# Feed-forward mixes queued elsewhere, later sums in the down product, constants and first weights moved: a hybrid decoder block on one core

## The chip, the cores and the metric

The kernel runs on one core of a Trainium2 chip. The metric is the device time of one execution in microseconds; before the change it is 1431.51 us, the median of three runs (1430.36 to 1434.9).

## The reference

One decoder block over T = 1040 positions (16 meta tokens and 1024 tokens), D = 1024, float32. `h` is normalized by `rmsnorm` and multiplied by `w_in`; the product is cut into `u`, `q`, `k`, `v` and two gates. `u` runs through an S5 state-space mixer, `q`, `k`, `v` through differential attention with four heads, both are gated, added and projected by `w_o`. What the change touches most is the feed-forward part:

```python
hn = rmsnorm(h, norm1_g); proj = hn @ w_in
...
h = h + mixed @ w_o
up = rmsnorm(h, norm2_g) @ w_up            # 1024 -> 2 * 2816
a, b = up[..., :D_FF], up[..., D_FF:]
c = a_pad[:, 0:seq] * conv_w[0] + a_pad[:, 1:seq+1] * conv_w[1] + a_pad[:, 2:seq+2] * conv_w[2] + conv_b
h = h + (gelu(c) * b) @ w_down             # 2816 -> 1024
```

## The kernel before

Every product is made of three matmuls per pair of tiles: both operands are split into a high part (fp32r, by ScalarE) and a remainder (by VectorE), and hi·hi, hi·lo and lo·hi are added in PSUM (`mm3_term`, L184, and `mm3`, L132). So each operand costs one ACTIVATE and one VectorE subtraction. `tt` (L94), `ts` (L98, L100), `stt` (L103) and `act` (L106) are helpers; L94 therefore stands for every two-operand VectorE or GpSimd instruction.

**Order.** The framework lays out each engine's instructions ahead of time by a simulated timeline: of the instructions whose inputs its model holds ready, the one written earlier goes first. On the chip each engine then runs its list in that order, and so does each DMA queue; all DMAs of this kernel are issued by SyncE (SP). `keep_in_program_order` puts an instruction behind the one last written for its engine; `issue_after(x)` puts what is written in its block, on the engine of `x`, behind `x`.

**Start** (`start`, L278). Eight row tiles of `hT` (128x1040) are loaded (L301), split with `g1` as scale into `hhi` and `hlo`, and the first two column blocks of `w_in` in pieces (L292). TensorE makes the 16 matmul groups of two u-blocks (six PSUM banks of eight). Then the squares of all eight rows are added into two accumulators `acc`, odd rows on GpSimd and even rows on VectorE; their sum goes through a ones matrix (`rms`, L155) and a chain of ScalarE and VectorE steps to the row `R1`, without which no u-bank can be emptied (`u_evict`). Two more u-blocks follow, then `small_params`, which makes small constants (lambda of the attention, scales) on VectorE, then the S5 constants (`ssm`, beginning with `exp_small` of `ldt`) beside the q, k and v blocks.

**Feed-forward up.** The product `w_up` is made in 2x2 block form with seven products instead of eight (Winograd's form of Strassen). A `Quad` is one set of seven: `part` 0 makes rows of `a` (columns of 258 and 256), `part` 1 rows of `b` (columns of 512). There are 11 quads of each part, in turn; `AHEAD` = 5 quads of part 1 have two of their products made before. `sums` makes four weight sums S1 to S4 on GpSimd from the loaded weights `wraw` (two buffers, L1210). `times` multiplies a result by its gelu row in `c`, on GpSimd; when four such are done, `mix` makes the block sums of the result (four subtractions on GpSimd, each followed by a store to DRAM, L1279 to L1288) for the down product. The rows `c` come from a pool of five.

**Feed-forward down** (`ffn_down`) is again in seven products of 11 steps. Each step loads an activation `act`, splits it (`bop`), splits the weight (`wop`), and makes 12 matmuls of 512 columns (L184). `then(f)` overwrites a block of the weight tile `wd` with a sum that a later product needs; in the first product this is `to_s3`, on VectorE.

Of the kernel before, what the change touches and what calls it, by code (L numbers as in the profile page):

```python
# [8 lines left out]
F32 = mybir.dt.float32  # L9
# [76 lines left out]
class Block:  # L86
# [100 lines left out]
    def build(self):  # L187
        nc, tc, a = self.nc, self.tc, self.a
        if True:
            P = lambda name, bufs=BUFS, **kw: Pool(tc, bufs, name, **kw)  # L190
            cst = self.cst = P("cst")
            self.dr = P("dr", space=bass.MemoryType.DRAM)
            self.wp = P("w")
            self.rowp = P("rows")
            self.tmp = P("tmp")
            self.A = P("A")

            par = cst.tile([128, NPAR], F32, name="par")
            self.par = par
            self.p = {k: par[:, s:e] for k, (s, e) in PAR.items()}  # L200
            self.ident = cst.tile([128, 128], F32, name="ident")
            self.ones = cst.tile([128, 128], F32, name="ones")
            nc.vector.memset(self.ones, 1.0)
            self.blk = cst.tile([128, 128], F32, name="blk")
            nc.vector.memset(self.blk, 0.0)
            nc.vector.memset(self.blk[0:64, 0:64], 1.0)
            nc.vector.memset(self.blk[64:128, 64:128], 1.0)

            d = lambda name, shape: self.dr.tile(shape, F32, name=name)
            self.d_qkv = [d(f"d_qkv{i}", [128, T]) for i in range(12)]  # L210
            self.d_gate = [d(f"d_gate{i}", [128, T2]) for i in range(16)]
            self.d_u = [d(f"d_u{i}", [GB, 16, CH, NJ]) for i in range(4)]
            self.d_y = [d(f"d_y{i}", [CH, 16, GB, NJ]) for i in range(4)]
            self.d_g = [d(f"d_g{i}", [128, T]) for i in range(3)]
            self.d_m1 = [d(f"d_m1{i}", [128, T2]) for i in range(8)]
            self.d_o = [d(f"d_o{i}", [128, T2]) for i in range(H)]
            self.d_h2 = [d(f"d_h2{i}", [128, SEQ]) for i in range(8)]
            self.d_p1, self.d_c11 = ([d(f"d_{n}{i}", [128, HW]) for i in range(AHEAD)] for n in ("p1", "c11"))
            self.d_act = [d(f"d_act{i}", [128, SEQ]) for i in range(NF)]
            self.d_t2, self.d_t3, self.d_t4 = ([d(f"d_t{n}{i}", [128, SEQ // 2]) for i in range(NQ)] for n in (2, 3, 4))  # L220

            x0 = self.x0 = P("X0", {})
            self.pp = P("ps0", {"mm": 8}, space=bass.MemoryType.PSUM)
            self.start()
            for i in (2, 3):
                self.u_block(i)
            self.small_params()
            x0.release()
            self.pp.release()
            self.pp = P("ps1", PBUFS[0], space=bass.MemoryType.PSUM)  # L230
            x = self.x = P("X1")
            ssm = self.ssm()
            step = lambda n: [next(ssm, None) for _ in range(n)]
            step(5)
            for h in range(H):
                for qk in range(2):
                    step(1)
                    self.qk_block(h, qk)
                step(1)
                self.v_block(h)  # L240
            fill = self.fillers()
            tc.keep_in_program_order(nc.scalar.preload_act_table_set(GELU))
            loaded = []
            for n, _ in enumerate(ssm):
                for z in loaded:
                    self.gelu_y(*z)
                loaded = [(i, self.load_branch(i)) for i in ((0, 1), (2,), ())[min(n, 2)]]
                spent = 0.0
                while spent < PRE:
                    spent += next(fill)  # L250
            self.run_later()
            x.release()
            self.pp.release()
            self.pp = P("ps3", PBUFS[1], space=bass.MemoryType.PSUM)
            self.Op = P("O")
            x = self.x = P("X3")
            with tc.manual_schedule(engines={mybir.EngineType.PE}):
                self.attention(fill)
            x.release()
            self.pp.release()  # L260
            self.pp = P("ps4", PBUFS[2], space=bass.MemoryType.PSUM)
            x = self.x = P("X4")
            self.att_out()
            self.w_o()
            x.release()
            self.Op.release()
            self.pp.release()
            self.pp = P("ps5", PBUFS[3], space=bass.MemoryType.PSUM)
            x = self.x = P("X6")
            self.ffn_up()  # L270
            x.release()
            x = self.x = P("X7")
            self.ffn_down()
            for z in (x, self.pp, self.A, self.tmp, self.rowp, self.wp, self.dr, self.cst):
                z.release()


    def start(self):  # L278
# [8 lines left out]
        for _ in range(2):  # L287
            ws.append([self.wp.tile([128, 8, 128], t, tag=n, name="w" + n) for t, n in ((F32, "raw"), (F32R, "hi"), (F32R, "lo"))])

        def weights(i, k0, k1):  # L290
            raw, hi, lo = (z[:, k0:k1] for z in ws[i])
            nc.sync.dma_start(out=raw, in_=a["w_in"][i][:, k0:k1])  # L292
            self.split(raw, hi, lo)

        for k in range(8):
            raw = self.x0.tile([128, T], F32, name=f"hraw{k}")
            hi = self.A.tile([128, T], F32R, tag="A", name="hhi")
            lo = self.A.tile([128, T], F32R, tag="A", name="hlo")
            for n, (c0, cn) in enumerate(C_U if k == 0 else [(0, T)]):
                cs = slice(c0, c0 + cn)  # L300
                nc.sync.dma_start(out=raw[:, cs], in_=a["hT"][k][:, cs])  # L301
                if k == 0 and n == 0:
                    nc.sync.dma_start(out=self.par[:, 0:8], in_=a["par"][:, 0:8])
                    weights(0, 0, 1)
                self.split(raw[:, cs], hi[:, cs], lo[:, cs], self.p["g1"][:, k:k + 1])
            if k == 0:
                weights(1, 0, 1)
                weights(0, 1, 4)
                weights(1, 1, 4)
            if k == 4:  # L310
                nc.sync.dma_start(out=self.par[:, 8:], in_=a["par"][:, 8:])
                nc.sync.dma_start(out=self.ident, in_=a["ident"])
# [14 lines left out]
        for k in range(8):  # L327
            if k < 2:
                self.act(accs[k], raws[k], AF.Square)
            else:  # L330
                self.act(raws[k], raws[k], AF.Square)
                self.tt(accs[k % 2], accs[k % 2], raws[k], ALU.add, eng=nc.gpsimd if k % 2 else None)
        self.E1 = self.rowp.tile([128, T], F32, tag="R", name="E1")
        self.tt(accs[0], accs[0], accs[1], ALU.add)
        self.R1 = self.rms_row(accs[0], T, self.E1)
        self.tap("R1", self.R1)
        for i in range(2):
            self.u_evict(i, ps[i])

# [145 lines left out]
    def small_params(self):  # L485

        p, cst = self.p, self.cst
        lam = p["lam"].rearrange("p (a d) -> p a d", a=4)
        pr = self.x0.tile([128, 2, 64], F32, name="lampr")
        self.tt(pr[:, 0], lam[:, 0], lam[:, 1], ALU.mult)  # L490
        self.tt(pr[:, 1], lam[:, 2], lam[:, 3], ALU.mult)
        s = cst.tile([128, 2], F32, name="lams")
# [17 lines left out]
    def ssm(self):  # L510
# [5 lines left out]
        sgn = q["sgn"]  # L516
        W = 4 * NG
        sm = lambda nm, n: x.tile([128, n], F32, name=nm)
        dt = self.exp_small(q["ldt"], NG, x)
        rr, th = sm("rr", W), sm("th", W)  # L520
        self.tt(rr[:, 0:NG], q["are"], dt, ALU.mult)
        self.tt(th[:, 0:NG], q["aim"], dt, ALU.mult)
# [504 lines left out]

    def ffn_up(self):
        nc = self.nc
        a0 = Quad(self, 0, 0)  # L1030
        bs = [Quad(self, 1, f) for f in range(AHEAD)]
        for q in bs:
# [14 lines left out]
        def whole(q):  # L1047
            q.load(2)
            q.sums()
            q.x12()  # L1050
            q.yz()

# [2 lines left out]
        for f in range(NQ):  # L1055
# [4 lines left out]
            if f < AHEAD:  # L1060
# [3 lines left out]
                    q.fetch()  # L1064
                q.load(2)
                q.sums()
                q.yz(True)
            else:
                q = Quad(self, 1, f)
                q.c = cs[f]  # L1070
                whole(q)

    def arow(self):
        pool, tag = (self.rowp, "R") if self.nar % 3 else (self.x, "ar")
# [20 lines left out]
    def ffn_down(self):  # L1095
# [25 lines left out]
        def to_s4(f):  # L1121
            self.tt(A12(f), A12(f), A21(f), ALU.subtract)

        def product(w, src, then=None):
            tiles = [self.psum("mm", [128, n]) for _ in range(4)]
            for f in range(NQ):
                i = count[0] % 13
# [11 lines left out]
                wh, wl = self.wop(w(f))  # L1139
                for m in range(4):  # L1140
                    self.mm3_term(tiles[m], (wh[:, m], wl[:, m], t[:, 0], t[:, 1]), f == 0, f == NQ - 1)
                if then is not None:
                    then(f)
            return tiles

        def quarter(pool, tag):
# [9 lines left out]
            nc.sync.dma_start(out=self.out[4 * i + m][:, n * half:n * half + n], in_=z)  # L1156

        act = lambda i, half: (lambda f: self.d_act[f + i * NQ][:, n * half:n * half + n])
        tiles = product(A11, act(0, 0), to_s3)
        u, v, w = quarter(self.A, "A"), quarter(self.A, "A"), quarter(x, "w")  # L1160
        for m, ps in enumerate(tiles):
            self.act(u[m], ps, AF.Copy)
# [28 lines left out]
class Quad:  # L1191


    def __init__(self, b, part, f):
        self.b, self.part, self.f, self.nc, self.x = b, part, f, b.nc, b.x
        self.c = None
        self.rows, self.done = [None, None], 0
        if part == 0:
            self.c0, self.n = 0, HW
            self.cuts = (slice(0, HW - 256), slice(HW - 256, HW))  # L1200
# [64 lines left out]
    def times(self, i, half, t):  # L1265
        b = self.b
        o = self.c[i][:, 512 * half:512 * half + 512]
        b.tt(o, o, t, ALU.mult, eng=self.nc.gpsimd)
        self.done += 1
        if self.done == 4:  # L1270
            self.mix()

    def mix(self):

        b, G, f = self.b, self.nc.gpsimd, self.f
        (r0, r1), h0, h1 = self.c, slice(0, 512), slice(512, 1024)
        t3 = self.temp("T")
        b.tt(t3, r1[:, h1], r0[:, h1], ALU.subtract, eng=G)
# [314 lines left out]
```

## Time and profile before

| | |
|---|---|
| median of 3 runs | 1431.51 us (1430.36 to 1434.9) |
| profiled execution | 1431.01 us, span of the trace 1429.2 us |
| busy: TensorE / weight loads / VectorE | 1404.2 (98%) / 1295.4 (91%) / 1029.2 us (72%) |
| busy: ScalarE / GpSimd | 631.9 (44%) / 371.8 us (26%) |
| TensorE clock granted | 0.995 of full, mean |

PE is the matmul engine, DVE is VectorE, ACT ScalarE, POOL GpSimd, SP SyncE; a small q marks an engine's sequencer or queue. Times in a trace count from the start of the span.

### The profile page before, as it was taken

How to read it: one execution, taken by the hardware profiler on the slowest of the kernel's cores; microseconds unless marked ns; L12 is line 12 of the kernel's file. 1: busy time of each engine (PE TensorE's matmuls, PEld its weight loads, DVE VectorE, ACT ScalarE, POOL GpSimd, SP SyncE). 2: the span in 40 equal slices, each digit the busy share in tenths (PEclk: the TensorE clock that was granted, in tenths of full speed). 3: DMA queues.
4: the chain of work that ended last, by engine and by line, in shares of the span. 5: the costliest groups of instructions: out<-in, count | busy, mean ns of one | idle time of the engine just before them, and what ended most of it. 6: DMA issues, size and time to landing. Idle time of an engine off the chain costs nothing.

```text
span 1429.2 us, 22918 instructions
## 1 busy us (share of the span) xinstructions
PE 1404.2 (98%) x8714; PEld 1295.4 (91%) x8714; DVE 1029.2 (72%) x2014; ACT 631.9 (44%) x1177; POOL 371.8 (26%) x242
## 2 busy tenths in 40 slices
PE   8999999999999999999999999999999999999998
PEld 7999999999999999889998999988889997788887
DVE  7998987345646577657366988888666779895574
ACT  6155555444545674433254633333333342444442
POOL 2000000121120111000220166676655557231030
PEclk9999999999999999999999999999999999999999
DMA  5333344471435334656433223333232337944331
GB/s 200 133 78 109 99 131 127 152 199 59 120 100 150 109 106 161 193 182 216 155 130 109 95 80 126 126 126 117 101 107 97 111 112 272 366 134 155 125 119 59
DMA packets 93917, 194.64 MB, mean 136 GB/s; under 512 B 27632, under 2 KB 36976, under 8 KB 93808
## 3 DMA queue, kind: packets, MB, share of 16 engines
q1 hardware_dynamic: 93376, 191.60, 41.5%
q8 instruction: 68, 1.11, 0.3%
q10 hardware_dynamic: 432, 1.60, 0.3%
q14 instruction: 41, 0.34, 0.1%
HBM read 134.88 MB, written 57.10 MB: 134 GB/s over the span
## 4 chain that ended last, share of the span: by engine, by line
PE 88%; DVE 6%; DMA 3%; issue 1%; ACT 1%; POOL 1%; SPq 0%; ACTq 0%; DVEq 0%; POOLq 0%
PE ps_mm L184 40%; PE ps_mm L132 37%; PE po L1463 3%; DVE wop L94 1%; PE s L1427 1%; PE wt L1472 1%; PE s L1428 1%; PE qss L377 1%; DMA wraw<-in_w_up 1%; DMA wd<-in_w_down 1%; PE vps L694 1%; PE yps L736 1%; PE yps L734 0%; PE km L672 0%; DVE crow L103 0%
## 5 line engine op out<-in xcount | busy, mean ns | idle before, releaser
L132 PE MATMUL ps_mm<-B,wop 128*128 128x512 f32 (+2 forms) x2772 | 436.9, 320 | 4.9 <-DVE u L94 3.9
L132 PEld LDWEIGHTS ps_mm<-B,wop 128*128 128x128 f32 x2772 | 395.3, 189 | 46.1 <-ACT wop L106 5.8
L184 PE MATMUL ps_mm<-bop,wop 128*128 128x512 f32 x924 | 216.0, 395 | 2.4 <-DVE bop L94 2.4
L184 PEld LDWEIGHTS ps_mm<-bop,wop 128*128 128x128 f32 x924 | 174.0, 189 | 44.2 <-DVE bop L94 3.3
L184 PE MATMUL ps_mm<-hhi,whi 128*128 128x342 f32 (+2 forms) x432 | 137.5, 329 | 2.5 <-ACT hhi L106 2.4
L184 PE MATMUL ps_mm<-hlo,whi 128*128 128x342 f32 (+2 forms) x432 | 138.8, 322 | 0.0
L184 PE MATMUL ps_mm<-hhi,wlo 128*128 128x342 f32 (+2 forms) x432 | 138.6, 322 | 0.0
L106 ACT ACTIVATE whi<-wraw 128x1024 fp32r<-128x1024 f32 (+3 forms) x62 | 62.1, 1004 | 125.9 <-PE ps_mm L184 46.1
L94 DVE TENSOR_TENSOR wop<-wraw,wop 128x512 fp32r<-128x512 f32 x88 | 97.1, 1108 | 23.5 <-ACT wop L106 23.1
L132 PE MATMUL ps_mm<-hhi,whi 128*128 128x348 f32 (+3 forms) x336 | 112.4, 335 | 0.0
L132 PE MATMUL ps_mm<-hhi,wlo 128*128 128x348 f32 (+3 forms) x336 | 110.0, 327 | 0.0
L132 PE MATMUL ps_mm<-hlo,whi 128*128 128x348 f32 (+3 forms) x336 | 109.2, 325 | 0.0
L94 POOL TENSOR_TENSOR wlo<-wraw,whi 128x1024 fp32r<-128x1024 f32 x18 | 45.2, 2512 | 224.3 <-ACT whi L106 224.3
L1429 DVE CUSTOM_DVE_ANT_0 S<-s,bias 128x348 f32<-128x348 f32 (+9 forms) x120 | 57.9, 484 | 59.6 <-PE s L1428 58.9
L106 ACT ACTIVATE bop<-act 128x512 fp32r<-128x512 f32 x77 | 48.4, 632 | 117.1 <-PE ps_mm L184 117.0
L94 DVE TENSOR_TENSOR wop<-S,wop 128x512 fp32r<-128x512 f32 x66 | 65.3, 990 | 48.1 <-ACT wop L106 48.1
L94 POOL TENSOR_TENSOR crow<-crow,T 128x512 f32<-128x512 f32 x44 | 70.7, 1620 | 97.5 <-DVE T L94 90.8
L106 ACT ACTIVATE wop<-wraw 128x512 fp32r<-128x512 f32 x88 | 54.1, 626 | 91.8 <-DMA wraw<-in_w_up 50.6
L94 DVE TENSOR_TENSOR bop<-act,bop 128x512 fp32r<-128x512 f32 x77 | 59.1, 769 | 46.1 <-ACT bop L106 46.1
L106 ACT ACTIVATE wop<-S 128x512 fp32r<-128x512 f32 x66 | 40.4, 626 | 110.3 <-POOL S L94 100.7
L184 PEld LDWEIGHTS ps_mm<-hhi,whi 128*128 128x128 f32 x432 | 80.6, 189 | 3.6 <-ACT hhi L106 3.0
L184 PEld LDWEIGHTS ps_mm<-hlo,whi 128*128 128x128 f32 x432 | 82.4, 191 | 0.7 <-DVE hlo L103 0.5
(316 smaller groups left out, 3015.4 us busy)
## 6 DMA issues: line engine op xcount, KB each, us to landing
wraw<-in_w_up SPq DMA_DIRECT2D x49, 512.0 KB, 3.6
wraw<-in_w_in SPq DMA_DIRECT2D x30, 512.0 KB, 4.2
d_act<-crow SPq DMA_DIRECT2D x22, 512.0 KB, 2.9
act<-d_act SPq DMA_DIRECT2D x44, 256.0 KB, 3.6
wd<-in_w_down SPq DMA_DIRECT2D x22, 512.0 KB, 7.4
d_t<-T SPq DMA_DIRECT2D x33, 256.0 KB, 4.2
act<-d_t SPq DMA_DIRECT2D x33, 256.0 KB, 3.0
d_gate<-gate SPq DMA_DIRECT2D x16, 513.0 KB, 4.8
```

The costliest lines, as they stand in the source:

```text
L94: (eng or self.nc.vector).tensor_tensor(out=out, in0=in0, in1=in1, op=op)
L106: self.nc.scalar.activation(out, in_, func, **kw)
L132: self.nc.tensor.matmul(out=ps, lhsT=w, rhs=b, start=(i == 0), stop=(i == n - 1))
L184: self.nc.tensor.matmul(out=ps, lhsT=w, rhs=b, start=first and i == 0, stop=last and i == 2)
L377: self.nc.tensor.matmul(out=ps, lhsT=self.blk, rhs=v, start=True, stop=True)
L694: pin(nc.tensor.matmul(out=ps[:, g], lhsT=d["VB"][:, g0 + g], rhs=d["u"][:, g0 + g, 0:NR], start=True, stop=True))
L736: nc.tensor.matmul(out=ps[:, g], lhsT=toe[:, g0 + g].rearrange("p n c -> p (n c)"), rhs=u[:, g0 + g], start=False, stop=True)
L1427: nc.tensor.matmul(out=ps, lhsT=q, rhs=self.KH[j][:, c0m:c0m + cm], start=True, stop=False)
L1428: nc.tensor.matmul(out=ps, lhsT=q, rhs=self.KL[j][:, c0m:c0m + cm], start=False, stop=True)
L1429: nc.vector.tensor_tensor_reduce(out=s[0:M, c0:c0 + cn], in0=ps[0:M, off:off + cn], in1=self.bias[0:M, b0 + c0:b0 + c0 + cn], scale=1.0, s ...
L1463: nc.tensor.matmul(out=po[0:M], lhsT=l, rhs=rr, start=(kk == 0), stop=(kk == nb))
L1472: nc.tensor.transpose(ps[:, r], w[:, NM + 128 * kk:NM + 128 * (kk + 1)], b.ident)
```

## The change

First, `mix` is no longer called when the fourth `times` of a quad is done: it is put into the list `mixes`, which is emptied after the next quad's `sums`, and at the end. Second, for the last quad of part 1 (`f == NQ - 1`) `times` and `mix` are on VectorE instead of GpSimd. Third, in the first down product `then(f)` comes five steps later (`lag`). Fourth, the six weight pieces of the first two blocks: four of them are issued by ScalarE's queue instead of SP's, and row 1 of `hT` is loaded and split in three pieces like row 0. Fifth, all additions into `acc` are on VectorE. Sixth, `small_params` is written behind the q, k and v blocks and a marker instruction, and `exp_small` of `ldt` behind a marker at the end of `R1`.

```diff
@@ build
             for i in (2, 3):
                 self.u_block(i)
-            self.small_params()
...
                 self.v_block(h)
+            last = tc.keep_in_program_order(nc.vector.memset(cst.tile([128, 1], F32, name="mark2"), 0.0)).ins
+            with tc.issue_after(last):
+                self.small_params()
@@ start
-        def weights(i, k0, k1):
+        def weights(i, k0, k1, eng=nc.sync):
             raw, hi, lo = (z[:, k0:k1] for z in ws[i])
-            nc.sync.dma_start(out=raw, in_=a["w_in"][i][:, k0:k1])
+            eng.dma_start(out=raw, in_=a["w_in"][i][:, k0:k1])
...
-            for n, (c0, cn) in enumerate(C_U if k == 0 else [(0, T)]):
+            for n, (c0, cn) in enumerate(C_U if k < 2 else [(0, T)]):
...
-                    weights(0, 0, 1)
+                    weights(0, 0, 1, nc.scalar)
...
-                weights(1, 0, 1)
-                weights(0, 1, 4)
-                weights(1, 1, 4)
+                weights(1, 0, 1, nc.scalar)
+                weights(0, 1, 4, nc.scalar)
+                weights(1, 1, 4, nc.scalar)
...
-                self.tt(accs[k % 2], accs[k % 2], raws[k], ALU.add, eng=nc.gpsimd if k % 2 else None)
+                self.tt(accs[k % 2], accs[k % 2], raws[k], ALU.add)
...
+        self.mark = self.tc.keep_in_program_order(nc.vector.memset(self.cst.tile([128, 1], F32, name="mark"), 0.0)).ins
@@ small_params
-        pr = self.x0.tile([128, 2, 64], F32, name="lampr")
+        pr = self.row(n=128, name="lampr").rearrange("p (a d) -> p a d", a=2)
@@ ssm
-        dt = self.exp_small(q["ldt"], NG, x)
+        with self.tc.issue_after(self.mark):
+            dt = self.exp_small(q["ldt"], NG, x)
@@ ffn_up
+        self.mixes = []
+        def mix():
+            while self.mixes:
+                self.mixes.pop(0)()
...
             q.sums()          # in whole(q), and for the quads ahead
+            mix()
...
+        mix()                 # at the end
@@ ffn_down
-        def product(w, src, then=None):
+        def product(w, src, then=None, lag=0):
...
-                if then is not None:
-                    then(f)
+                if then is not None and f >= lag:
+                    then(f - lag)
+            for f in range(NQ - lag, NQ):
+                then(f)
...
-        tiles = product(A11, act(0, 0), to_s3)
+        tiles = product(A11, act(0, 0), to_s3, 5)
@@ Quad
+        self.eng = self.nc.vector if part and f == NQ - 1 else self.nc.gpsimd
...
-        b.tt(o, o, t, ALU.mult, eng=self.nc.gpsimd)
+        b.tt(o, o, t, ALU.mult, eng=self.eng)
...
-            self.mix()
+            b.mixes.append(self.mix)
...
-        b, G, f = self.b, self.nc.gpsimd, self.f
+        b, G, f = self.b, self.eng, self.f
```

## Rows read from the trace of the kernel before

**Rows 1.** The page, busy time of each engine, share of the span, instructions.
```profile
PE 1404.2 (98%) x8714; PEld 1295.4 (91%) x8714; DVE 1029.2 (72%) x2014; ACT 631.9 (44%) x1177; POOL 371.8 (26%) x242
```

**Rows 2.** Waits of TensorE: who, for whom: us in total, times, longest.
```profile
PE ps_mm L132 <- DVE u L94: 3.9, 3, 1.6
...
PE rms L155 <- DVE acc L94: 3.7, 1, 3.7
PE ps_mm L184 <- DVE bop L94: 2.4, 2, 2.1
```

**Rows 3.** Windows of the start: stretch, length, busy by engine, clock, DMA share, GB/s.
```profile
8.60:10.94 2.34, 0.00 (x0) 0.00 (x1) 0.33 (x2) 1.21 (x2) 0.00 (x0) 1.00 1.01 395
10.94:15.43 4.49, 4.49 (x17) 4.15 (x18) 3.77 (x5) 4.49 (x6) 0.00 (x0) 0.62 1.01 394
...
32.80:36.50 3.70, 0.01 (x2) 0.01 (x1) 3.49 (x10) 1.06 (x1) 2.19 (x2) 0.89 0.12 47
36.50:40.33 3.83, 3.83 (x7) 1.87 (x7) 3.29 (x6) 1.63 (x4) 0.00 (x0) 0.50 0.42 132
40.33:42.50 2.17, 2.17 (x9) 2.17 (x9) 1.92 (x10) 1.92 (x6) 0.00 (x0) 0.50 0.93 268
42.50:46.00 3.50, 3.50 (x23) 3.50 (x23) 3.50 (x14) 0.44 (x2) 0.00 (x0) 1.00 0.25 97
```

**Rows 4.** Timeline of SP's queue at the start: start, us, engine, line, instruction.
```profile
4.49 0.91 SPq L301 DMA_DIRECT2D hraw<-in_hT  x2
```

**Rows 5.** Timeline of ScalarE at the start; in brackets idle before, and releaser.
```profile
0.73 1.28 ACT L281 ACT_TABLE_LOAD   x1 [0.73 <-PEq L1584]
...
9.73 1.16 ACT L106 ACTIVATE hhi<-hraw,par 128x1040 fp32r<-128x1040 f32 x1 [1.41 <-DMA hraw<-in_hT]
```

**Rows 6.** Timeline of VectorE, 14 to 51 us.
```profile
18.18 2.35 DVE L98 TENSOR_SCALAR glub<-par 128x4 f32<-128x4 f32 x1
...
25.71 2.41 DVE L103 SCALAR_TENSOR_TENSOR ex_f<-ex_k,ex_x 128x2 f32<-128x2 f32 x1
28.04 1.29 DVE L103 SCALAR_TENSOR_TENSOR hlo<-hraw,par,hhi 128x1040 fp32r<-128x1040 f32 x1
...
31.75 3.34 DVE L103 SCALAR_TENSOR_TENSOR ex_p<-ex_p,ex_f 128x2 f32<-128x2 f32 x6
...
35.20 1.24 DVE L94 TENSOR_TENSOR acc<-acc,acc 128x1040 f32<-128x1040 f32 x1
...
46.63 4.09 DVE L94 TENSOR_TENSOR u<-ps_mm,R 128x352 f32<-128x352 f32 x6
```

**Rows 7.** Timeline of GpSimd at the start, the first of three such.
```profile
18.06 2.44 POOL L94 TENSOR_TENSOR acc<-acc,hraw 128x1040 f32<-128x1040 f32 x1 [17.61 <-ACT hraw L106]
```

**Rows 8.** Timeline of TensorE, ones matmuls of the second norm.
```profile
762.87 1.03 PE L969 MATMUL rms<-acc,ones 128*128 128x256 f32 x4
```

**Rows 9.** Timeline of GpSimd over one round of the two parts, 1055 to 1095 us.
```profile
1063.48 1.29 POOL L94 TENSOR_TENSOR S<-wraw 128x512 f32<-128x512 f32 x1 [1.49 <-DMA wraw<-in_w_up]
...
1073.41 1.62 POOL L94 TENSOR_TENSOR T<-crow 128x512 f32<-128x512 f32 x1
...
1084.07 1.29 POOL L94 TENSOR_TENSOR S<-wraw 128x512 f32<-128x512 f32 x1 [2.39 <-DMA wraw<-in_w_up]
```

**Rows 10.** Windows where the up product hands over to the down product.
```profile
1207.00:1214.00 7.00, 6.69 (x30) 5.13 (x28) 6.78 (x9) 2.94 (x5) 5.09 (x4) 1.00 1.04 410
1214.00:1219.10 5.10, 3.04 (x12) 2.17 (x12) 5.10 (x4) 1.15 (x2) 4.94 (x4) 1.00 0.79 314
1219.10:1223.50 4.40, 4.36 (x12) 3.46 (x13) 4.40 (x6) 1.15 (x2) 1.13 (x1) 0.61 0.86 281
```

**Rows 11.** Timeline of VectorE, 1200 to 1225 us.
```profile
1207.27 1.49 DVE L94 TENSOR_TENSOR wd<-wd 128x512 f32<-128x512 f32 x1 [0.22 <-DMA wd<-in_w_down]
...
1217.31 1.78 DVE L94 TENSOR_TENSOR bop<-act,bop 128x512 fp32r<-128x512 f32 x1
...
1221.90 0.68 DVE L94 TENSOR_TENSOR bop<-act,bop 128x512 fp32r<-128x512 f32 x1
```

More of the change, by code (lines that the diff above doesn't have):

```diff
@@ L1071, in ffn_up @@
                 whole(q)
+        mix()
     def arow(self):
```

## Prediction

> **What bounds the kernel now.** I read the engines' busy times first. TensorE is busy 1404.2 us of the 1429.2 us span, so it was idle for 25.0 us [rows 1]: no edit that spares another engine can be worth more than those 25 us and the time TensorE ran at the lower clock. Next I read who TensorE waited for. The waits that lie where the diff works are the norm's wait for `acc`, 3.7 us, the down product's for `bop`, 2.4 us in two waits, and three waits in the up product for an emptied bank, 3.9 us together [rows 2]. Windows then show the clock beside the idle time. [...] At the hand-over to the down product the idle time is 2.06 us, followed by a window at 0.61 [rows 10]. [...] Everywhere else TensorE is full, so a time won at the start is kept to the end unless a later stage spends it.
>
> **The start: who is late for the norm.** The norm's six matmuls begin at 36.50, when the last addition into `acc` (35.20, 1.24 us) is done. In the 17.0 us of VectorE from 18.18 to 35.20 [rows 6] it does two additions into `acc` (1.24 each, by the last one), four `hlo` and one weight remainder of nearly the same size (1.29 each): 2.5 + 6.4 = 8.9 us. The other 8.1 us are `small_params`, which does next to no arithmetic: `glub`, 128x4, took 2.35 us, `ex_f`, 128x2, 2.41, and the six `ex_p` together 3.34. They are long where GpSimd runs an addition of 2.44 us or more (the first begins at 18.06, `glub` at 18.18) [rows 6, 7]. There are three such additions on GpSimd.
>
> The change takes away the 8.1 us (constants moved, no GpSimd addition beside them) and adds three additions on VectorE, 3 x 1.24 = 3.7. Net -4.4 us: the norm starts at 36.50 - 4.4 = 32.1.
>
> **Does TensorE reach the norm by then?** Its two u-blocks end at 32.80 before. The first stall, 2.34 us, waits for row 1: its load is issued at 4.49, behind row 0 and four weight pieces, and its split of 1.16 us starts on the whole row at 9.73 [rows 4, 5]. Four weight issues off SP's queue are 4 x 0.46 = 1.8 us (two issues took 0.91 [rows 4]); two more row issues come in, 0.9 us, but the first third of row 1 is out 1.9 us earlier and is split in about a third of 1.16 us. Row 1 then feeds TensorE at about 7.5, before the end of row 0's matmuls. Row 2 comes hardly earlier, as the transfers ran at a share of 1.01 from 8.60 on [rows 3]; I leave 1.2 us of wait for it. The stall shrinks by 1.1 us, and 4.49 x 0.38 = 1.7 us of lower clock mostly with it: u-blocks end near 30. None of it counts twice: the norm is gated by `acc` at 32.1 either way, and what the earlier row buys is that TensorE is there before it.
>
> From the norm on: at half clock six matmuls and their tail took 3.83 us [rows 3]. At full clock four of 256 columns took 1.03 [rows 8], so six of 346 cost 1.03 x 6/4 x 346/256 = 2.1. The next u-block starts at 32.1 + 2.1 = 34.2 instead of 40.33, a gain of 6.1, and 2.17 us at clock 0.50 cost 1.1 more [rows 3]: 7.2 without crediting earlier loads to `acc`. If the wait of 2.1 us that is left (30 to 32.1) lowers the clock all the same, 4.4 remains. A window at lower clock followed the wait of 2.34 us [rows 3], and the up product's longest wait is 1.6 [rows 2]; 2.1 lies between, but `acc` may also be earlier, as VectorE has row 1 sooner. I take 6.5, nearer to the full clock. Two free banks hold 2 x 24 matmuls of 3.50/23 us = 7.3 us of work [rows 3], to 41.5; the first bank was emptied 46.63 - 36.50 = 10.1 us after the norm's start [rows 6], less 1.7 of faster matmuls: 40.5. So the wait for a bank stays hidden, with 1 us in hand. Bounds of the start: +0 (loads or ScalarE gate `acc` just as late) to -9.2 (`acc` 2 us earlier still, full clock).
>
> `small_params` behind the v blocks costs nothing: some 25 tiny instructions, at a place where VectorE has idle time (72% busy over all [rows 1]); its results are read only in attention and later. `exp_small` of `ldt` behind `R1` keeps 15 small instructions out of R1's chain; it begins no later than before, since R1 itself is earlier.
>
> [...] ScalarE begins with a table load of 1.28 us at 0.73 [rows 5]. [...]
>
> **The mixes.** Their new place in the program order changes nothing that I can find. On GpSimd the next quad's sums already start at 1063.48, ten us ahead of the mix at 1073.41; the sums behind it, at 1084.07, belong to the quad after next and follow the mix in the new order too. Both sums waited for their weight load, 1.49 and 2.39 us, not for the mix [rows 9]. So 0 for ten quads. Bounds: -3.9, if the three bank waits [rows 2] go, to +15 (the rival below).
>
> **The hand-over.** VectorE is full there: 5.10 of 5.10 us [rows 10]. `bop` took 1.78 us beside GpSimd's last mix and 0.68 four us later without it, and a `wd` sum ahead of it waited for its load and then took 1.49 [rows 11]. In the change GpSimd is idle, `wd` sums like this one, three of them ahead of the late `bop`, come later, and eight instructions of 0.68 = 5.4 us come in. Between 1207 and 1219.1 VectorE did 9 + 4 = 13 instructions in 11.9 us [rows 10]; then there are 13 - 3 + 7 (one of the eight is due earlier) = 17 of 0.68, 11.6 us: it fits, barely. What can be won is 0.34 + 2.06 of idle time (the 2.4 of rows 2) and 4.40 x 0.39 = 1.7 of lower clock [rows 10], 4.1 us. I take 3.5. Bounds: -4.1, and +1.3 if all eight stand ahead of one `bop` (5.4 against 4.1).
>
> [...] The rows say that the neighbour costs VectorE 1.1 us per instruction, more than the 0.68 it costs to do the work itself. [...]
>
> **Sum.** 1431.0 (profiled execution: span 1429.2 and 1.8 around it) - 6.5 - 3.5 + 0 = 1421.0. The median of the runs shown is 0.5 above that execution, so I forecast between 1421.0 and 1421.5: 1421.2.
>
> **Rivals.**
> A, half of it: the start is gated by ScalarE's splits and squares, or by the rows' arrival, as soon as VectorE is free, and VectorE does the last mix in one block. For it: ScalarE was busy all of 10.94 to 15.43 [rows 3]. Against it: it waits for VectorE later. 3 + 0.8 (3.5 less four instructions of 0.68): 1431.5 - 3.8 = 1427.7.
> B, nothing: the gain moves into the wait for a bank (1 us in hand is little) and the late `bop`: 1430.5.
> C, more: the three bank waits go as well, since the planner lays the up product out anew: 1421.2 - 3.9 = 1417.3.
> D, slower: the mixes do get behind the sums, and sums wait for their loads. Then `mix` comes later by four sums (4 x 1.3 and more) and a wait of 2.4, some 8 us [rows 9], and holds its rows of `c`, five slots in all, until its stores have landed. Once that is longer than the slack to the next quad's rows (I estimate one or two us above 8 from a round of 39.7 us), ScalarE stops at the row and the weight splits behind it stop too: 1.5 us per hand-over, like the longest wait of 1.6 now [rows 2], at ten of them: 1421.2 + 15 = 1436.2. Against it: on GpSimd the order is what it was.
>
> **Chances.** Forecast (1418 to 1424.5) 0.53, A 0.18, B 0.10, C 0.10, D 0.09. Range 1415.5 to 1430.2, which leaves out most of D, a part of B and little below. 0.3% (4.3 us) is about what a measurement of this kernel can tell from no change, that is 1427.2: faster has the forecast, C and over half of A, 0.74; same has the rest of A and B, 0.17; slower D, 0.09.
>
> **What would show it.** Right: the norm's wait for `acc` under 2 us and its matmuls before 33 us; no slow window after 12 us, or a shorter one; the late `bop` at 0.68 us and no slow window there; GpSimd's order of sums and mixes as before and the three bank waits still there. Wrong: the first u-block after the norm later than 37 us, new waits of TensorE between the quads, or the last mix as one block ahead of a `bop`.

## The result, and the profile after

The changed kernel takes 1421.2 us, the median of four runs (1420.68 to 1422.89), beside 1432.64 us of the kernel before on the same chip: ratio 0.9934 [0.9921, 0.9946], with the 95% interval in brackets, as in all that follows. The prediction was 1421.2. Later, beside other runs, it was 1421.77 to 1430.46: 0.9939 [0.9924, 0.9953]. A ratio is taken over the undisturbed runs, so it is not just that of the medians.

The page of the kernel after, busy time of each engine (its span is 1420.9 us; answers to [rows 1]):

```profile
PE 1400.1 (99%) x8714; PEld 1292.7 (91%) x8714; DVE 1026.7 (72%) x2029; ACT 631.2 (44%) x1179; POOL 348.5 (25%) x231
```

Waits of TensorE, us in total, times, longest (answers to [rows 2]):

```profile
PE ps_mm L132 <- DVE u L94: 3.6, 4, 1.4
PE s L1443 <- DVE m L1445: 3.4, 4, 1.4
...
PE ps_mm L184 <- DVE bop L94: 1.5, 1, 1.5
PE rms L155 <- DVE rms_v L100: 1.5, 1, 1.5
...
PE ps_mm L184 <- ACT hhi L106: 0.9, 2, 0.5
...
PE rms L155 <- DVE acc L94: 0.2, 1, 0.2
```

The norm's wait for `acc` is down from 3.7 to 0.2. A wait of 1.5 for `rms_v` stands in its place, one of 1.5 for `bop` is left of two of 2.4, and `s`, in attention, is new among the long ones.

Windows of the kernel after, with the columns of [rows 3] (PE, PEld, DVE, ACT, POOL, clock, DMA share, GB/s), at the start, in attention and at the hand-over:

```profile
8.60:10.94 2.34, 1.85 (x11) 1.40 (x11) 1.58 (x4) 2.14 (x5) 0.00 (x0) 1.00 1.00 363
10.94:15.43 4.49, 4.43 (x28) 4.14 (x28) 3.09 (x5) 4.49 (x6) 0.00 (x0) 1.00 1.03 392
...
36.50:40.33 3.83, 3.83 (x26) 3.83 (x25) 2.81 (x12) 0.99 (x2) 0.00 (x0) 1.00 0.35 128
...
469.70:473.10 3.40, 3.21 (x10) 3.07 (x11) 2.15 (x9) 1.15 (x2) 0.00 (x0) 0.50 0.02 5
1207.00:1212.00 5.00, 3.52 (x16) 2.56 (x15) 5.00 (x10) 1.45 (x3) 0.00 (x0) 1.00 1.03 411
```

TensorE's first stall is 0.5 us of the 2.34 in this window instead of all of it (with two short waits at 6 to 7 us, which are new, it is 1.1 in all), and the clock stays at 1.00 where it was 0.62 and 0.50 [rows 3]. At the hand-over the clock stays up too, with 1.48 us idle and VectorE full. But for the last microseconds, the one stretch at 0.50 is in attention, where before there was none (1.00 from 455 to 482).

Timeline of TensorE at the norm (start, us, what ran, and in brackets the idle time before it and its releaser), and of VectorE (answers to [rows 6]):

```profile
30.75 1.43 PE L155 MATMUL rms<-acc,ones 128*128 128x348 f32 x4 [0.19 <-DVE acc L94]
33.66 0.85 PE L155 MATMUL rms<-acc,ones 128*128 128x346 f32 x2 [1.48 <-DVE rms_v L100]
34.17 0.50 PE L132 MATMUL ps_mm<-hhi,whi 128*128 128x352 f32 x1
...
42.56 0.40 PE L132 MATMUL ps_mm<-hhi,whi 128*128 128x344 f32 x1 [0.41 <-DVE u L94]
```

```profile
29.45 1.24 DVE L94 TENSOR_TENSOR acc<-acc,acc 128x1040 f32<-128x1040 f32 x1
30.61 2.57 DVE L94 TENSOR_TENSOR wlo<-wraw,whi 128x1024 fp32r<-128x1024 f32 x2
33.09 0.94 DVE L100 TENSOR_SCALAR rms_v<-rms 128x348 f32<-128x348 f32 x2
```

The norm begins at 30.75 (36.50 before), its last two matmuls wait for a PSUM bank, which VectorE empties (`rms_v`) only after two weight remainders (`wlo`), and the next u-block begins at 34.17 (40.3 before).

To see where the time came from I compare when the same matmul starts in two traces: matmul number n, in the order of the list, starts so many us earlier than before. One profiled execution each, on several chips:

| n, and its start before | 500 (95) | 2800 (444) | 3200 (506) | 6000 (918) | 7800 (1209) | 8100 (1283) |
|---|---|---|---|---|---|---|
| changed kernel | 7.0 | 6.5 | 4.2 | 4.9 | 5.6 | 8.4 |
| the same, another execution | 7.0 | 6.5 | 6.3 | 6.6 | 5.5 | 8.6 |
| start alone | 7.8 | 7.3 | 5.1 | 4.1 | 4.4 | 5.4 |
| last quad alone | 0.9 | 0.6 | 0.3 | -3.0 | -2.0 | 2.5 |
| before's lists again | 1.4 | 1.4 | 1.6 | 2.4 | 2.8 | 3.7 |
| additions alone | 2.8 | 3.1 | 2.6 | 2.7 | 2.8 | 3.2 |
| constants alone | 2.9 | 2.9 | 2.9 | 2.2 | 0.2 | 1.1 |
| constants and additions | 4.0 | 2.9 | 3.3 | 4.3 | 4.6 | 5.7 |
| loads alone | -0.4 | -0.9 | -3.7 | -2.5 | -3.0 | -0.4 |
| sums pinned, in a block | 7.7 | 7.2 | 6.6 | 8.3 | 8.9 | 6.2 |
| sums pinned, spread | 6.7 | 6.2 | 5.7 | 6.8 | 7.8 | 10.9 |

The changed kernel wins 7.0 at the start, loses 2.2 in attention in one execution and 0.2 in the other, and wins 2.8 or 3.1 at the hand-over. The fifth line is the warning: the same instruction lists as before, and 3.7 us apart. (The 26 runs of the kernel before that were timed beside it lie between 1427.92 and 1434.86 us.)

### The profile page after: what moved, and what is told of

It reads as the page before. It is cut to its first block, busy times and chain, and to the rows that moved or that the text cites. A ratio compares the mean times of both kernels' runs of the same rounds, so it can differ in the third digit from the quotient of the medians.

```text
span 1420.9 us, 22933 instructions
## 1 busy us (share of the span) xinstructions
PE 1400.1 (99%) x8714; PEld 1292.7 (91%) x8714; DVE 1026.7 (72%) x2029; ACT 631.2 (44%) x1179; POOL 348.5 (25%) x231
## 4 chain that ended last, share of the span: by engine, by line
PE 83%; DVE 7%; DMA 4%; POOL 3%; ACT 2%; issue 1%; SPq 0%; POOLq 0%; ACTq 0%; DVEq 0%
PE ps_mm L184 40%; PE ps_mm L132 31%; PE po L1479 3%; POOL crow L94 2%; DVE wop L94 2%; DMA wraw<-in_w_up 1%; PE wt L1488 1%; PE s L1443 1%; PE s L1444 1%; PE qss L380 1%; POOL S L94 1%; DMA wraw<-in_w_in 1%; DVE crow L103 1%; DVE u L94 1%; DMA orow<-d_o 1%
## 5 line engine op out<-in xcount | busy, mean ns | idle before, releaser
L94 POOL TENSOR_TENSOR crow<-crow,T 128x512 f32<-128x512 f32 x40 | 63.9, 1615 | 90.8 <-DVE T L94 84.1
```

What stands on the lines that cost most here:

```text
L94: (eng or self.nc.vector).tensor_tensor(out=out, in0=in0, in1=in1, op=op)
```

## The experiments

Each was run in five rounds beside the kernel before.

**The start alone**: the parts of the diff in `build`, `start`, `small_params` and `ssm`; the feed-forward as before.

> The five edits of the start alone (constants behind the v blocks, exp_small of ldt behind R1, additions into acc on VectorE, first weight issues on ScalarE's queue, row 1 in thirds); the feed-forward as before. Theory: the start gives 6.5 us, and what the changed kernel showed near 466 us (TensorE idle 1.4 us, then a stretch of 3.4 us at a granted clock of 0.50) belongs to the start's edits and costs about 2 of them in every execution: ratio about 0.997, 1428 us, with the slow stretch at 470 in the profile. Rival: that stretch was an accident of one execution: 1426 us (0.9955), no slow stretch there. Second rival: the feed-forward's edits carry more of the whole than the traces say: above 1429.

1424.85 us, ratio 0.9952 [0.9939, 0.9966], so 6.9 of 1430.85 us. The stretch at half clock near 470 was there (granted clock 0.51 from 469.0 to 472.5), as the theory said, but the start is worth more than the theory allowed: the price is the first rival's (0.9955), though its sign, no slow stretch, did not come. The second rival is out.

**The last quad alone**:

```diff
+        self.eng = self.nc.vector if part and f == NQ - 1 else self.nc.gpsimd
...
-        b.tt(o, o, t, ALU.mult, eng=self.nc.gpsimd)
+        b.tt(o, o, t, ALU.mult, eng=self.eng)
...
-        b, G, f = self.b, self.nc.gpsimd, self.f
+        b, G, f = self.b, self.eng, self.f
```

> Only the last quad's four products and its mix on VectorE. Theory: the whole gain at the hand-over is this edit's: the late bop takes about 0.68 us instead of 1.78, no stretch at half clock near 1220 us, one wait of TensorE of about 1.7 us for bop as in the changed kernel: 2.8 us less, ratio 0.998, 1429.8 us. Rival 1 (VectorE and GpSimd gain nothing by the swap, only the later sums of the down product help): 0 to -1, 1432. Rival 2 (the block of eight instructions ahead of a bop costs more without the later sums): +1.3, 1434.

1428.27 us, 0.9982 [0.9971, 0.9992]: 2.6 us, as the theory had it, both rivals out. One thing was not as expected: TensorE doesn't wait for `bop` at all. Timeline of TensorE in this run, then in the changed kernel:

```profile
1199.82 9.45 PE L132 MATMUL ps_mm<-B,wop 128*128 128x512 f32 x40
1209.11 27.16 PE L184 MATMUL ps_mm<-bop,wop 128*128 128x512 f32 x117
```

```profile
1201.49 6.59 PE L184 MATMUL ps_mm<-bop,wop 128*128 128x512 f32 x28
1209.56 6.71 PE L184 MATMUL ps_mm<-bop,wop 128*128 128x512 f32 x28 [1.48 <-DVE bop L94]
```

In the changed kernel, which has the start's gain, TensorE comes 7.6 us earlier to the product's first operand (1201.49 against 1209.11), but VectorE comes only 5.9 earlier to the remainder `bop` of the third (1208.83 against 1214.77): VectorE sets the time here, and a part of what was won before is given back.

**The mixes' new place and the later sums alone**, GpSimd as before:

```diff
-            self.mix()
+            b.mixes.append(self.mix)
...
                 q.sums()
+                mix()
...
-        tiles = product(A11, act(0, 0), to_s3)
+        tiles = product(A11, act(0, 0), to_s3, 5)
```

> Only the mixes behind the next quad's weight sums and the down product's first sums five operands later. The built program holds the same instructions in the same order on every engine as the kernel before. Theory: no difference, ratio 1.000 within 0.0015. Rival (a different wait or buffer in the same order): 1 to 2 us faster, as the prediction would have the later sums, or slower.

1430.02 us, 0.9996 [0.9984, 1.0007]: no difference, the rival is out. In the two traces every engine has the same instructions in the same order. The reason for that is argued, not shown: the planner takes an instruction when its inputs are ready, and neither edit changes that. What the run shows beside it is the clock. Waits of TensorE in this run, then two windows of it:

```profile
PE rms L155 <- DVE acc L94: 3.7, 1, 3.7
...
PE ps_mm L184 <- DVE bop L94: 2.9, 3, 2.1
...
PE ps_mm L184 <- ACT hhi L106: 1.7, 1, 1.7
```

```profile
10.94:15.43 4.49, 4.38 (x28) 4.09 (x27) 3.54 (x5) 3.95 (x6) 0.00 (x0) 1.00 1.03 394
...
36.50:40.33 3.83, 3.70 (x9) 1.79 (x8) 3.78 (x9) 2.40 (x6) 0.00 (x0) 0.56 0.55 161
40.33:42.50 2.17, 2.17 (x15) 2.17 (x14) 1.38 (x8) 1.60 (x5) 0.00 (x0) 0.99 0.94 315
...
1214.00:1219.00 5.00, 2.94 (x14) 2.17 (x12) 5.00 (x5) 1.06 (x4) 3.26 (x3) 1.00 0.81 275
```

The norm's wait is the same 3.7 as in [rows 2], and `bop`'s is longer, yet the clock is 1.00 at the hand-over and falls behind the norm for a shorter time than in [rows 3] (0.56 and 0.99 in the two windows that are both at 0.50 there). (It is 1.00 after the first stall too, but that wait was 1.7 us here and 2.36 before.) So whether a wait is followed by half clock differs from execution to execution of one list: at the hand-over a wait of 2.06 us was followed by 0.61 before [rows 10], and by 1.00 here (mean from 1195 to 1230, where before it is 0.95). At the hand-over six of the traces (before, the start alone, this run, additions alone, constants alone, constants and additions) have a wait of 2.0 to 2.1 us, and only two of them (before and additions alone, 0.95 each from 1195 to 1230) have half clock behind it. What decides it, no run shows.

**The additions alone**:

```diff
-                self.tt(accs[k % 2], accs[k % 2], raws[k], ALU.add, eng=nc.gpsimd if k % 2 else None)
+                self.tt(accs[k % 2], accs[k % 2], raws[k], ALU.add)
```

> Only the three additions into acc from GpSimd to VectorE; the constants stay where they were. Theory: constants' instructions on VectorE were long only while GpSimd's addition ran (glub began 0.12 us after it and ended with it); without it each takes about 0.15 us, so 8.1 us become about 2.5 and 3.7 are added: the norm's matmuls begin at 36.5 - 5.6 + 3.7 = 34.6, TensorE waits about 1.8 us instead of 3.7: 2 to 5 us faster (5 if the clock stays up), 1428 to 1430.5. Rival: their length is their own (many tiny instructions at a late place): norm at 40.2, 3.7 us and more slower, 1436.

1428.14 us, 0.9983 [0.9974, 0.9991]: 2.4 us, in the theory's range, the norm at 34.82 (34.6 expected). Timeline of VectorE in this run:

```profile
17.89 0.16 DVE L98 TENSOR_SCALAR glub<-par 128x4 f32<-128x4 f32 x1
...
29.02 0.16 DVE L103 SCALAR_TENSOR_TENSOR ex_f<-ex_k,ex_x 128x2 f32<-128x2 f32 x1
...
32.39 1.23 DVE L94 TENSOR_TENSOR wlo<-wraw,whi 128x1024 fp32r<-128x1024 f32 x1 [1.99 <-ACT whi L106]
33.53 1.24 DVE L94 TENSOR_TENSOR acc<-acc,acc 128x1040 f32<-128x1040 f32 x1
```

The same two instructions took 2.35 and 2.41 beside GpSimd [rows 6]. Their length was a wait. That the norm came where it was expected is chance, though. The constants cost VectorE 1.1 us up to `acc` here, counted from start to start, not 2.5, and the squares were added by 30.33; but in this run's list a weight remainder stands ahead of the last addition, and VectorE waited 1.99 us for its input.

**The constants alone**:

```diff
-            self.small_params()
             x0.release()
...
+            with tc.issue_after(last):
+                self.small_params()
...
+        with self.tc.issue_after(self.mark):
+            dt = self.exp_small(q["ldt"], NG, x)
```

> Only the constants: small_params behind the v blocks, exp_small of ldt behind R1; the three additions stay on GpSimd, the loads as before. Theory: the constants' 8.1 us on VectorE alone held acc, and without them acc is ready when TensorE ends its two u-blocks (32.8): no wait for the norm, no stretch at half clock behind it, 3.7 + 1.7 = 5.4 us less: 1425.5, ratio 0.996. Rival: GpSimd's additions (2.4 to 3.5 us each) then lengthen other VectorE instructions or end last themselves: norm at about 34.5, 2 us less, 1429.

1427.97 us, 0.9986 [0.9975, 0.9998], 2.0 us, the norm at 34.34: the rival, to the number; the theory fell. Timelines of GpSimd and of VectorE in this run:

```profile
18.64 2.95 POOL L94 TENSOR_TENSOR acc<-acc,hraw 128x1040 f32<-128x1040 f32 x1 [18.19 <-ACT hraw L106]
...
29.71 3.29 POOL L94 TENSOR_TENSOR acc<-acc,hraw 128x1040 f32<-128x1040 f32 x1 [2.35 <-ACT hraw L106]
```

```profile
19.64 3.05 DVE L103 SCALAR_TENSOR_TENSOR hlo<-hraw,par,hhi 128x1040 fp32r<-128x1040 f32 x1 [0.36 <-ACT hhi L106]
...
33.04 1.24 DVE L94 TENSOR_TENSOR acc<-acc,acc 128x1040 f32<-128x1040 f32 x1 [2.29 <-POOL acc L94]
```

Once the constants were gone, GpSimd's addition held `hlo` instead: 3.05 for 1.29, ending 1.1 after the addition (18.64 + 2.95 = 21.59). And GpSimd's own last addition became the latest input of `acc`. So the constants were the victims and the additions the cause: with the constants gone, the next VectorE instruction became the victim.

The ends agree with that: `glub` ended at 20.53, GpSimd's addition at 20.50 [rows 6, 7]. Why the one is held by the other, no run shows.

**Constants and additions**: the last two diffs together, loads as before.

> Constants moved and the three additions on VectorE, loads as before. Theory: TensorE's u-blocks, ending at 32.8, are the gate already without the additions, so this is within 1 us of the constants alone, 1425 to 1426, and what is left to the whole start (1424.85) belongs to the loads: about 1 us. Rival (constants and additions gain only together): 3 us faster than the constants alone.

1426.25 us, 0.9981 [0.9961, 1.0002]; the interval is too wide to place it against the two alone. The trace says more. Timeline of TensorE in this run:

```profile
32.67 1.33 PE L155 MATMUL rms<-acc,ones 128*128 128x348 f32 x4
35.51 0.85 PE L155 MATMUL rms<-acc,ones 128*128 128x346 f32 x2 [1.51 <-DVE rms_v L100]
...
45.58 0.40 PE L132 MATMUL ps_mm<-hhi,whi 128*128 128x344 f32 x1 [1.57 <-DVE u L94]
```

The norm begins without a wait when the u-blocks end, so TensorE is the gate, as the theory put it. But 1.57 us go into the wait for a bank, as rival B of the prediction had it, and only 2.9 to 4.0 are left at n = 500 to 2800.

**The loads alone**:

```diff
-            for n, (c0, cn) in enumerate(C_U if k == 0 else [(0, T)]):
+            for n, (c0, cn) in enumerate(C_U if k < 2 else [(0, T)]):
...
-                    weights(0, 0, 1)
+                    weights(0, 0, 1, nc.scalar)
```

> Only the first weights on ScalarE's queue and row 1 in thirds. Theory: TensorE's wait for row 1 at 8.3 us shrinks from 2.3 to under 1 and the u-blocks end near 30, but the norm still waits for acc until 36.5: the wait there grows by what is won, 0 us, ratio 0.999 to 1.001 (-1.7 at most, where the stretch at half clock at 12 us was paid). Rival 1: earlier rows bring acc forward too: 2 us faster. [...]

1431.47 us, 1.0007 [0.9993, 1.0020]: nothing, as the theory said. Waits of TensorE, then its timeline in this run:

```profile
PE ps_mm L184 <- DVE hlo L103: 2.0, 2, 1.8
```

```profile
37.80 3.83 PE L155 MATMUL rms<-acc,ones 128*128 128x348 f32 x6 [4.41 <-DVE acc L94]
```

The wait at the norm has grown from 3.7 to 4.4, but not for the theory's reason. The u-blocks end at 33.39 (37.80 less 4.41), not near 30 and not earlier than the 32.80 before: what the earlier rows won went into a new wait of 1.8 us for an `hlo`, which stood on VectorE behind the 2.35 us of `glub`. Beside the other two parts the same loads let the norm begin at 30.30 (the start alone) instead of 32.67, which is 2.4 us, and the bank wait is 0.41 in the changed kernel, not 1.57. This is read from single traces, not timed by itself.

**The sums really later**: the changed kernel, with `then(f - lag)` held behind `lo`, the VectorE instruction that makes the lower half of operand f; what is left behind the last.

```diff
...
-                    then(f - lag)
...
+                    with self.tc.issue_after(lo):
+                        then(f - lag)
...
```

> The changed kernel, and the down product's first sums pinned behind the lower half of the operand five later, so that nine wd sums really leave VectorE's list ahead of the first operands. Theory: TensorE's wait of 1.66 us for bop was VectorE's backlog, six sums of 0.60 lie ahead of that bop; it goes: 1.7 us faster than the changed kernel, ratio to the kernel before 0.992, with no wait over 0.9 us at the hand-over. Rival 1: the wait is the mix's block, three instructions ahead of the bop: it stays. Rival 2: the six sums that are left to the end of the first product stand in one block ahead of the next operands: a new wait of up to 2 us there, no gain.

1426.13 us, 0.9970 [0.9958, 0.9982], slower than the changed kernel. The wait of 1.48 for the third operand is down to 0.52, so it was the sums ahead of it, and rival 2 came, at nearly twice its price. Timelines of VectorE and of TensorE in this run:

```profile
1228.01 3.69 DVE L94 TENSOR_TENSOR wd<-wd 128x512 f32<-128x512 f32 x6
```

```profile
1234.16 4.21 PE L184 MATMUL ps_mm<-bop,wop 128*128 128x512 f32 x9 [3.57 <-DVE bop L1152]
```

Six sums in one block hold the second product's operands, and TensorE idles 3.57 us and then runs slow (granted clock 0.72 from 1228 to 1240).

**The change again**, on the chip of the next three:

> The changed kernel once more, beside the three that start from it: ratio to the kernel before 0.9934, 1421 us if before is at 1430.5. The profile shows whether the stretch at half clock near 470 us belongs to the program (theory: TensorE idle 1.4 to 1.6 us at 465 each time, the stretch in some executions only) or was one execution's (rival: no idle time there).

1421.77 us, 0.9939 [0.9924, 0.9953]. TensorE waits at 466 again, 0.81 us (1.41 in the first profile), without half clock behind it: the wait is the program's, and the stretch came in one of two executions. The theory has it, but for the size. The length may matter too: in all the traces here the stretch near 470 follows this wait where it was 1.30, 1.41 or 2.62 us, and in none of the eleven where it was 1.20 or less. No run settles that.

**The sums spread**: three operands later, the last three behind the second product's first operands, so that no block is left (`LAGD` = 3).

```diff
-        tiles = product(A11, act(0, 0), to_s3, 5)
+        tiles = product(A11, act(0, 0), to_s3, LAGD)
...
-        for m, ps in enumerate(product(A21, lambda f: self.d_t3[f])):
+        for m, ps in enumerate(product(A21, lambda f: self.d_t3[f], to_s3, LAGD - NQ)):
```

> The changed kernel with the down product's first sums pinned three operands later, one behind each operand's lower half, and the last three behind the first operands of the second product, so that no block of sums is left. Theory: the wait for bop at the hand-over (1.66) goes as in the run with the sums pinned five later, and the new wait of 3.75 us at 1230 (six sums in a row, 3.69) doesn't come: 1.7 to 2.3 us faster than the changed kernel, 1419, ratio to before 0.992. Rival: VectorE is full for the whole stretch from 1195 to 1250 (0.60 per instruction without a gap in the changed kernel), so the wait only moves: 0.

1422.46 us, 0.9952 [0.9937, 0.9967]: no gain. Timeline of TensorE in this run:

```profile
1199.72 31.37 PE L185 MATMUL ps_mm<-bop,wop 128*128 128x512 f32 x134
1231.99 4.22 PE L185 MATMUL ps_mm<-bop,wop 128*128 128x512 f32 x17 [0.90 <-DVE bop L1153]
```

The rival holds: the wait of 1.06 at 1209 in the run of the change again has become one of 0.90 at 1232. That VectorE has no room in this stretch, so that its backlog is paid somewhere, fits both runs.

**The gates' stores from ScalarE's queue**, on top of that:

```diff
-            self.nc.sync.dma_start(out=self.d_gate[i], in_=x)
+            self.nc.scalar.dma_start(out=self.d_gate[i], in_=x)
```

> As the run with the sums spread, and the gates' stores issued on ScalarE's queue right behind the activation that writes them, not on SP's behind two loads. Theory: yt's activation at 464.7 waits for the slot that the gate's store (issued 458.72, 0.66 after the gate was done) still reads; VectorE's gate and the freeing of TensorE's bank stand behind it. The store 0.66 earlier takes the idle time at 466 from 1.4-1.6 to about 0.8: 0.7 us faster, and 1.7 more where the stretch at half clock goes: 1417.5 to 1418.5. Rival: the slot waits for something else (the glu weight's load): no change there, and 16 issues on ScalarE cost up to 1 us.

1423.49 us, 0.9953 [0.9936, 0.9970]: no gain in time, but the releaser is settled. Timeline of ScalarE in this run, then in the changed kernel:

```profile
458.01 0.33 ACTq L456 DMA_DIRECT2D d_gate<-gate  x1
...
463.98 2.21 ACT L107 ACTIVATE yt<-yraw 128x1040 f32<-128x1040 f32 x1 [3.17 <-DMA d_gate<-gate]
```

```profile
464.73 2.19 ACT L106 ACTIVATE yt<-yraw 128x1040 f32<-128x1040 f32 x1 [3.76 <-DMA wraw<-in_w_ssm_out]
```

On SP's queue the profile put the wait down to a weight load; with the store on its own queue it names the store. `yt` waits for the buffer that the gate's store reads, VectorE's next gate for `yt`, and TensorE's bank for VectorE. The chain follows the issue: 458.72 in the changed kernel, 458.03 when it ran again, 458.01 here, and TensorE's wait is 1.41, 0.81, 0.78. With SP free at the right moment the store is as early from SP, so there was little to win.

**The norm's evictions ahead of the weight remainders**, on top of both (`second_v` is the norm's second eviction):

```diff
-            for i in (2, 3):
-                self.u_block(i)
+            self.u_block(2)
+            with tc.issue_after(self.second_v):
+                self.u_block(3)
```

> As the run before it, and the fourth u-block's weight remainder pinned behind the norm's first two evictions on VectorE, which moves both remainders (2.57 us) behind them. Theory: the norm's last matmuls no longer wait 1.5 us for rms_v (33.66 in the changed kernel, about 32.2 here); the next u-block then waits for its own remainder, ready at about 33.9 instead of 34.5: 0.6 us faster, and R1 about 1.2 earlier, so that the wait for a bank at 42.6 (0.4) goes too: 1 us. Rival: the planner lays the stages behind it out anew, and the difference is of either sign and more than 1 us.

1426.93 us, 0.9973 [0.9960, 0.9987], slower: the rival. The wait for `rms_v` goes, but the planner lays out the later stages anew (TensorE's own order differs from the run before it). Waits of TensorE in this run:

```profile
PE ps_mm L133 <- DVE u L95: 7.6, 7, 1.8
...
PE ps_mm L187 <- DVE gate L95: 2.0, 1, 2.0
```

Seven waits for a bank (four in the run before it, 4.3 us) and a new one of 2.0 take more than was won. No version here beats the changed kernel.

## Why the prediction was right, and where it was not

**The bound.** Right that a time won at the start is mostly kept (7.0 us at n = 500, 5.6 and 5.5 at 7800), and that the waits named were the ones to win. Wrong in taking the slow stretch behind each long wait as its fixed price: run again, the same lists had the same waits at the norm and at the hand-over, and 3.4 us at half clock instead of 13.7 (without the last microseconds). The lower clock was counted as certain; behind the wait at the hand-over it came in two of six traces.

**The start, -6.5.** Measured 6.9 [4.9, 8.7] in the runs, 7.0 in the trace. The mechanism was right: GpSimd's additions made the constants long (`glub` 2.35 us beside one, 0.16 without). The next u-block was put at 34.2 and began at 34.17, but that is luck: two errors cancel. `acc` came 1.4 earlier than 32.1 (also without the loads, 29.40 + 1.24, so it isn't the earlier row), because the constants were mis-sized. From the same `hlo` to the last addition VectorE took 19.8 us before (15.36 to 35.20) and 14.2 after (15.22 to 29.45), 5.6 less and not 4.4: counted from start to start the constants held it for 9.2 us from 16.57 on, where the prediction has 8.1 from 18.18. And the last two matmuls waited 1.48 for `rms_v`, which was not foreseen. Row 1 was put at 7.5 on TensorE and came at 9.86: ScalarE split it only from 9.23 on, behind a weight split that waited 0.72 for its load. The stall still shrank from 2.36 to 1.1, near the 1.2 that the prediction left, in other places. The bank wait was to be hidden with 1 us in hand: it shows, with 0.41, in this execution and is under 0.15 in the other.

**The loads** were taken as no gain by themselves (right, 1.0007 alone) but as what brings TensorE to the norm in time: right beside the other parts, not alone, where `glub` held them up.

**The table load** did not hold back the weights' issues. Timeline of ScalarE in the kernel after:

```profile
0.73 1.28 ACT L283 ACT_TABLE_LOAD   x1 [0.73 <-PEq L1600]
0.76 1.35 ACTq L294 DMA_DIRECT2D wraw<-in_w_in  x3
```

ScalarE's queue issued three weights from 0.76 to 2.11, while the load ran from 0.73 to 2.01.

**The mixes, 0.** Right, and the three bank waits stay, as the rows of GpSimd's order had said: rival C, which would have won them, and rival D, which wanted another order, are both out: the lists are equal when these two edits stand alone.

**The hand-over, -3.5.** 2.6 [1.1, 4.1] in the runs with the last quad alone, 2.8 and 3.1 in the traces of the whole. The late `bop` at 0.68 and the clock at 1.00 came as said. Two terms failed. One is "three of them ahead of the late `bop`, come later": the lag moves no instruction, so VectorE had 20 instructions to do where 17 would fit "barely". Alone the 20 still fitted, at 0.60 from one start to the next: the last quad alone has no wait. But with the start's gain TensorE came 7.6 us earlier and VectorE 5.9, and 1.5 us of wait stayed, which the sum of two separate parts left out. It stands one operand earlier than the late `bop`: between the second and the third remainder `bop` VectorE has eight `wd` sums and six of the eight instructions taken from GpSimd. The other is the 1.7 us of lower clock, which the same wait brought in two of six traces. That VectorE gained by taking GpSimd's work is shown: later sums alone gave 0 and the swap alone 2.6.

**Not foreseen** was the loss in attention, 2.2 us in one execution and 0.2 in the other.

**The sum.** Start 6.9 and last quad 2.6 make 9.5; the whole is 9.5 [7.7, 11.3] by its first ratio and 8.7 by its second. Rivals A (1427.7) and B (1430.5) are out by the intervals. That the median is the forecast to the digit is luck: the intervals are about 4 us wide, and the start gave more and the hand-over less than their terms.

## What to carry to other kernels

Tiny instructions that took microseconds were victims here (`glub` 2.35 us, 0.16 without GpSimd's addition): look at what the neighbouring engine runs at that moment and move that, since moving the victims away made the next instruction one. Where a planner lays out the work, writing a call elsewhere may change nothing; compare the built lists before giving the edit a price. Parts that gate one another need not add: here 2.4, 2.0 and 0 alone stand beside 6.9 [4.9, 8.7] together. That difference is near the edge of the noise, but the traces name what took over as the gate in each part. And a stretch at half clock seen once behind a wait is no fixed price of that wait: behind the one at the hand-over it came in two of six traces.

## What the runs showed of the hardware that was not expected

The same lists ran 1427.3 and 1431.0 us when profiled. Of the 3.7 us between them 1.4 had come by n = 500 and 0.9 came at the hand-over, where the stretches at half clock of the slower one lie; the rest came where neither has one, so it is not the clock's. A wait of 1.41 us was followed by half clock in one execution (0.50 for 3.40 us), one of 2.1 in another by none (1.00).

VectorE's instructions of 128x512 begin every 0.60 us when none waits (six in 3.69), though each alone is shown as 0.68: a full stretch holds more of them than their durations say, and sums of durations, as in the prediction, come out too long.
